# A trunk block on one core: loads of the first stage, one scale row, and the border to the FFN rearranged

## The chip, the core and the metric

The kernel runs on one core of a Trainium2 chip. The core's engines are named as the profile names them: PE (matrix unit; PEld is its weight load), DVE, ACT and POOL (elementwise engines), and SP, which issues most DMAs. The metric is the device time of one execution in microseconds (us), over three executions of each kernel. Lower is better.

## The reference

One block of a diffusion transformer, in float32, on 1024 latent tokens `x` and 256 context tokens `ctx` of width D = 1024.

```python
mod = silu(c) @ w_ada + b_ada                 # 6 x 1024: shift and scale 1, gate 1, shift and scale 2, gate 2
hc  = rmsnorm(ctx, g_pre_mix) * (1 + csc1) + csh1      # same weights, vector c_ctx
hl  = rmsnorm(x,   g_pre_mix) * (1 + sc1) + sh1
zc, zl = hc @ w_in, hl @ w_in                 # columns: q, k, v, dec, og, f, rx, rg
states = context_mixer(zc)                    # final states of GLA and RG-LRU
yl  = latent_mixer(zl, states)                # GLA (512) | 2-D DFT (256) | conv + RG-LRU (256)
x   = x + gt1 * rmsnorm(yl @ w_out, g_post_mix)
hf  = rmsnorm(x, g_pre_ffn) * (1 + sc2) + sh2
x   = x + gt2 * rmsnorm((silu(hf @ w_gate) * (hf @ w_up)) @ w_down, g_post_ffn)   # inner width 2816
```

## The kernel before

**Products.** Each float32 operand is split into a high and a low part of a reduced format (`split`: an ACT cast, line 91, and a subtraction, line 92), and `mm3` (lines 84 to 86) adds up three matmuls, high by high, high by low and low by high. So every product costs three matmuls of up to 512 columns.

**Memory and order.** Tiles come from two pools of fixed slots (`pg`, 43 of 4 KB a partition, and `hp`, 13 of 2 KB); a tile that takes a slot waits until its last user is done. A scheduler orders the instructions of each engine; an engine runs its own list strictly in that order and waits where an operand is late. All plain loads (`load`, line 70) stand in one list on SP; ACT issues the transfers of intermediate results.

**First stage.** `w_ada` holds the shift and scale of the first norm in its first 2048 columns. `ada_half(h)` (L145) loads one half of both, eight loads of 512 KB in rows of 2 KB, and multiplies them by silu of the conditioning in 64 matmuls 32x256 (L154, `ada_ps`). `columns(h)` turns the result into per-channel columns (L200 `ada_pc`, then `Acol`, `Bcol`). Both need all of a half. `transposed` (L181, `xT_ps`) turns normed tokens so that channels lie on partitions, and `modulate` scales and shifts them and splits them into `hc` (context) or `hl` (latent, two halves of 512 tokens). The order is: context normed, half 0, `hc` of its channels, the context's v (`zvc`), half 1, its k (`zkc`), then latent half 0, the context's rx (`zc`), and then the latent tokens' products: z of v for half 0 (`zn`, columns 288), half 1 modulated, z of k and rx for half 0 (`z`), v for half 1, z of k for half 1, and so on. The weights of k (`w_k`) and v (`w_v`) are split with POOL doing the subtraction.

**Rows.** `ada_row` (L664) makes one row of `mod` for all tokens: eight loads of 512 KB, each followed by a multiply-add on DVE (L671, `ada_acc`), then matmuls that sum over partitions and spread the row (L682, `row_ps`); `times_row` multiplies by a gain. It serves gate 1 (`rows[0]`) and scale 2 (`sc2`); shift 2 becomes a column instead (L676, `col_ps`). `ada_step(n)` lets n steps run at a given place of the program.

**Border to the FFN.** The FFN's three weights are multiplied by a seven-product scheme: operands a11, a12 (tokens' quarters), s1, s2, s3, s4, a22 (sums of quarters, made by `sums(n)` for block pairs n = 0 to 3) against sums of weight quarters (`t_split`). Per inner block f of 22, `first(f)` makes two of the products (24 matmuls of 512 columns, which need a11, a12 and the gate's split `b1s[f]`, made by `ff_gate(f)` and `ff_b1(f)`), and `rest(f)` the other five (60 matmuls). Eight output blocks of 128 tokens come out of `w_out` (`o_ps`); each is normed, gated, normed again (`xr`, `xn`, L1025 and L1034), transposed (L1042, `x_tr`) into `hx`, and put into the operands (`put`, a cast and a subtraction L937). POOL does part of the sums (L1071, L1074) and of the subtractions. Before the loop over f the order is sums(0), sums(1), first(0), first(1), transposes of the last block, sums(2), first(2), sums(3), the weights of f = 0, and then `rest(0)`.

Of the kernel before, what the change touches and what calls it, by code (L numbers as in the profile page):

```python
# [16 lines left out]
P = 128  # L17
# [21 lines left out]
def tile_trunk(ctx: ExitStack, tc: tile.TileContext, A: dict):  # L39
# [101 lines left out]
    sp2, sm4 = sm("sp2", 4), sm("sm4", 4)
    V.tensor_scalar_mul(sp2, sp, 2.0)
    V.tensor_scalar_mul(sm4, sp, -4.0)

    def ada_half(h):  # L145

        ps = (aux if h else mm)("ada_ps")
        for k in range(KB):
            raw = pg((P, 2, 512), name="ada_raw")
            load(raw, A["w_ada"][k * P:(k + 1) * P, 0:2 * D].rearrange("p (i n) -> p i n", i=2)[:, :, h * 512:(h + 1) * 512])  # L150
            for i in range(2):
                for j in range(2):
                    q = 32 * (2 * i + j)
                    PE.matmul(ps[q:q + 32, 0:256], s32[:, k, :], raw[:, i, j * 256:(j + 1) * 256], start=k == 0, stop=k == KB - 1)  # L154
        return ps

    Acol = pool.tile([P, KB, 2], F32, name="Acol")
    Bcol = pool.tile([P, KB, 2], F32, name="Bcol")
# [26 lines left out]
    def modulate(kps, which, hi_of, lo_of):  # L185

        for kk, ps in kps:
            f = hp((P, ps.shape[1]), name="xT")
            i = S.activation(f, ps, AF.Identity, bias=Bcol[:, kk, which:which + 1], scale=Acol[:, kk, which:which + 1])
# [4 lines left out]
    def columns(h, ps):  # L194

        sb = hp((P, 256), name="ada_sb")
        S.copy(sb, ps[:, 0:256])
        pc = (aux if h else mm)("ada_pc")[:, 0:16].rearrange("p (m q) -> p m q", q=8)
        for m in range(2):
            PE.matmul(pc[:, m], sb[:, m * P:(m + 1) * P], sel, start=True, stop=True)  # L200
        pcv = pc.rearrange("p m (i j w) -> p i j m w", i=2, j=2)

        def col4(c0):
            return sml[:, c0 + 4 * h:c0 + 4 * h + 4].rearrange("p (j m) -> p j m", j=2).unsqueeze(3).to_broadcast([P, 2, 2, 2])

        Av, Bv = (t[:, 4 * h:4 * h + 4, :].rearrange("p (j m) w -> p j m w", j=2) for t in (Acol, Bcol))
        V.tensor_add(Av, pcv[:, 1], col4(S_BSC))
        V.scalar_tensor_tensor(Av, Av, 1.0, col4(S_GPM), op0=ALU.add, op1=ALU.mult)
        V.tensor_add(Bv, pcv[:, 0], col4(S_BSH))

    load(cm, A["cmat"])
    cb = [row_block(A["ctx"], i * P) for i in range(2)]
    ada_ps = ada_half(0)
    for xb in cb:
        norm(xb)
    cT = list(transposed(cb))
# [74 lines left out]

    raws = w_N_load([(C_V, 256), (C_DEC, 32)])
    columns(0, ada_ps)
    hc = [[pg((P, 4, TC), F32R, f"hc{s}{i}") for i in range(2)] for s in range(2)]

    def mod_c(h):
        return modulate(cT[4 * h:4 * h + 4], 1, lambda kk: hc[0][kk // 4][:, kk % 4, :], lambda kk: hc[1][kk // 4][:, kk % 4, :])

    mod_c(0)
    w_v = [w_N_split(raws, G)]  # L300
    w_k_raw = [w_T_load(C_K)]
    zvc = [mm("zvc") for _ in range(2)]
# [62 lines left out]
    for m in range(2):  # L365
        v0_parts(zdt_c, m, vNc[0][:, m, :], zvc[m])
# [1117 lines left out]
```

## Time and profile before

| | before |
|---|---|
| runs | 1134.39, 1131.55, 1133.83 us; median 1133.83 |
| profiled execution | 1134.18 us, span 1132.4 us in the trace |
| busy PE, DVE, ACT, POOL | 1078.5, 810.4, 490.2, 83.6 us |
| mean granted TensorE clock | 0.979 of full speed |

The profile shows one execution. Its span is 1.8 us shorter than the time measured for it; times in the trace count from the span's start. The granted clock is given as a share of 2.4 GHz, so 0.50 in a stretch is the level of 1.2 GHz throughout.

### The profile page before, as it was taken

To read this page: it belongs to the slowest core of one execution; us is meant where nothing else is said; L and a number is where in the kernel's file an instruction comes from. 1 tells how busy PE (TensorE), PEld (TensorE's weight loads), DVE (VectorE), ACT (ScalarE), POOL (GpSimd) and SP (SyncE) were. 2 spreads that over 40 slices of the span, in tenths; PEclk is the share of its full clock that TensorE was granted. 3 is DMA by queue.
4 is the path that set the end of the run, shared out by engine and by line. 5 is a ranking of instruction groups with operands and counts; after the bars stand their busy time and mean duration, and the time that the engine had idled before them with its cause. 6 is when DMAs were issued, how large, how long until landed. Compare 5 with 4: busy or idle time off the path is not lost.

```text
span 1132.4 us, 15040 instructions
## 1 busy us (share of the span) xinstructions
PE 1078.5 (95%) x5547; PEld 900.1 (79%) x5547; DVE 810.4 (72%) x1370; ACT 490.2 (43%) x931; POOL 83.6 (7%) x93
## 2 busy tenths in 40 slices
PE   4899998999899999959999999999999999999997
PEld 2799896776689888838878888888888888888886
DVE  3474698477588466797879777768777668967794
ACT  3452675466373355663314332333323247554251
POOL 2210000103100011370000000000000000000100
PEclk8899999999999999979999999999999999999999
DMA  9802312222427222361283242424232468767572
GB/s 328 306 20 67 120 38 56 48 56 71 167 75 243 75 93 94 112 167 57 93 276 106 78 136 84 121 75 139 85 114 81 157 218 315 267 216 231 181 283 75
DMA packets 119970, 156.42 MB, mean 138 GB/s; under 512 B 8276, under 2 KB 70996, under 8 KB 119896
## 3 DMA queue, kind: packets, MB, share of 16 engines
q1 hardware_dynamic: 106536, 128.72, 34.9%
q10 hardware_dynamic: 13360, 26.75, 7.0%
q8 instruction: 43, 0.70, 0.3%
q14 instruction: 31, 0.25, 0.1%
HBM read 124.50 MB, written 28.57 MB: 135 GB/s over the span
## 4 chain that ended last, share of the span: by engine, by line
PE 83%; DVE 6%; DMA 4%; ACT 3%; issue 2%; POOL 1%; SPq 0%; DVEq 0%; POOLq 0%; ACTq 0%
PE prod L84 11%; PE prod L85 11%; PE prod L86 11%; PE dn L85 6%; PE dn L84 6%; PE dn L86 6%; PE z L84 3%; PE z L85 3%; PE z L86 3%; PE o_ps L85 3%; PE o_ps L86 3%; PE o_ps L84 3%; PE zn L85 3%; PE zn L86 3%; PE zn L84 2%; DMA wraw<-in_w_in 2%
## 5 line engine op out<-in xcount | busy, mean ns | idle before, releaser
L85 PE MATMUL dn<-dr,dl 128*128 128x512 f32 (+1 forms) x319 | 121.8, 382 | 0.0
L86 PE MATMUL dn<-dr,dl 128*128 128x512 f32 (+1 forms) x319 | 121.8, 382 | 0.0
L84 PE MATMUL dn<-dr,dl 128*128 128x512 f32 (+1 forms) x319 | 118.7, 382 | 0.0
L85 PE MATMUL zn<-w_lo,hl 128*128 128x256 f32 (+1 forms) x256 | 74.1, 292 | 0.0
L84 PE MATMUL zn<-w_hi,hl 128*128 128x256 f32 (+1 forms) x256 | 73.2, 289 | 0.0
L86 PE MATMUL zn<-w_hi,hl 128*128 128x256 f32 (+1 forms) x256 | 72.9, 288 | 0.0
L84 PE MATMUL prod<-a,b_hi 128*128 128x512 f32 x176 | 69.5, 395 | 1.4 <-ACT b_hi L91 1.4
L84 PEld LDWEIGHTS dn<-dr,dl 128*128 128x128 f32 x319 | 60.0, 188 | 11.7
L85 PE MATMUL prod<-a,b_hi 128*128 128x512 f32 x176 | 69.3, 393 | 0.0
L86 PEld LDWEIGHTS dn<-dr,dl 128*128 128x128 f32 x319 | 60.0, 188 | 11.7
L85 PEld LDWEIGHTS dn<-dr,dl 128*128 128x128 f32 x319 | 60.0, 188 | 11.5
L84 PE MATMUL prod<-s,wb_hi 128*128 128x512 f32 x176 | 68.9, 391 | 0.0
L86 PE MATMUL prod<-s,wb_lo 128*128 128x512 f32 x176 | 68.5, 389 | 0.0
L85 PE MATMUL prod<-s,wb_hi 128*128 128x512 f32 x176 | 68.5, 389 | 0.0
L86 PE MATMUL prod<-a,b_lo 128*128 128x512 f32 x176 | 67.9, 390 | 0.0
L84 PE MATMUL z<-hl,w_hi 128*128 128x512 f32 x160 | 65.5, 409 | 1.0 <-ACT on L605 1.0
L85 PE MATMUL z<-hl,w_hi 128*128 128x512 f32 x160 | 64.0, 400 | 0.0
L86 PE MATMUL z<-hl,w_lo 128*128 128x512 f32 x160 | 63.8, 399 | 0.0
L1189 ACT CAST dl<-h 128x512 fp32r<-128x512 f32 x77 | 47.8, 620 | 35.7 <-issue 20.6
L1190 DVE TENSOR_TENSOR dl<-h,dl 128x512 fp32r<-128x512 f32 x77 | 53.3, 692 | 13.6 <-ACT dl L1189 13.6
L1122 ACT CAST b<-wf_raw 128x512 fp32r<-128x512 f32 x22 | 13.7, 622 | 113.6 <-PE prod L86 105.7
L85 PE MATMUL o_ps<-wo_lo,yh 128*128 128x512 f32 x128 | 49.9, 392 | 0.0
(368 smaller groups left out, 2800.8 us busy)
## 6 DMA issues: line engine op xcount, KB each, us to landing
ada_raw<-in_w_ada SPq DMA_DIRECT2D x48, 512.0 KB, 6.3
h<-hd SPq DMA_DIRECT2D x77, 256.0 KB, 5.0
wd_raw<-in_w_down SPq DMA_DIRECT2D x77, 256.0 KB, 4.8
hd<-c ACTq DMA_DIRECT2D x55, 256.0 KB, 2.0
wf_raw<-in_w_gate SPq DMA_DIRECT2D x25, 512.0 KB, 3.9
wf_raw<-in_w_up SPq DMA_DIRECT2D x22, 512.0 KB, 4.4
wraw<-in_w_in SPq DMA_DIRECT2D x16, 512.0 KB, 4.6
xb<-in_x SPq DMA_DIRECT2D x8, 512.0 KB, 8.1
```

Of the source, the lines that this page charges most:

```text
L84: PE.matmul(out, lh, rh, start=start, stop=False)
L85: PE.matmul(out, lh, rl, start=False, stop=False)
L86: return PE.matmul(out, ll, rh, start=False, stop=stop)
L1122: S.copy(hi, u[:, 4:8])
L1189: S.copy(t[:, 0, :], raw)
L1190: V.tensor_sub(t[:, 1, :], raw, t[:, 0, :].bitcast(F32))
```

## The change

**Start.** Latent half 0 comes first. Its four blocks of x are issued on ACT's list; shift and scale are handled by blocks of 128 channels, blocks 0 and 1 alone (rows of 512 bytes), blocks 2 to 7 by pairs (rows of 1 KB); the k and rx weights come in four parts (`w4`, two loads each, rows of 1 KB). As soon as a block of channels is modulated, z of k and rx is multiplied with it (`z_block`, 12 matmuls of 512 columns). The context's work moves behind v of latent half 1. No weights are split on POOL.

```diff
+    xb0 = [pg(name="xb") for _ in range(4)]
+    for i, xb in enumerate(xb0):
+        nc.scalar.dma_start(xb, A["x"][i * P:(i + 1) * P, :])
...
+    def ada_load(b, n=1):
+        parts = [[], []]
+        for i in range(2):
+            c, kn = i * D + b * P, KB // n
+            for k0 in range(0, KB, kn):
+                raw = pg((P, kn, n * P), name="ada_raw")
+                load(raw, A["w_ada"][k0 * P:(k0 + kn) * P, c:c + n * P].rearrange("(k p) n -> p k n", p=P))
...
+    def ada_part(raws):
+        ps = aux("ada_ps")
         for k in range(KB):
...
             for i in range(2):
...
+                g = 32 * (2 * i + k % 2)
+                PE.matmul(ps[g:g + 32, 0:P], s32[:, k, :], raws[k][i], start=k < 2, stop=k >= KB - 2)
...
+    (a_raw[0],), w4_raw[0], (a_raw[1],) = ada_load(0), w4_load(0), ada_load(1)
+    for q in range(1, 4):
+        a_raw[2 * q], a_raw[2 * q + 1] = ada_load(2 * q, 2)
+        w4_raw[q] = w4_load(q)
+    v_raws = w_N_load([(C_V, 256), (C_DEC, 32)])
...
+    w4_split()
+    for b in range(KB):
+        kps = [next(x0_T)]
+        columns(b, ada_part(a_raw.pop(b)))
+        modulate(kps, 0, lambda kk: hl[0][0][kk // 2][:, kk % 2, :], lambda kk: hl[1][0][kk // 2][:, kk % 2, :])
+        if b:
+            z_block(b - 1)
+        if b % 2:
+            w4_split()
+    softplus()
+    w_v = [w_N_split(v_raws)]
+    z_block(KB - 1)
```

On PE, the matmuls of `ada_ps` stood in two long blocks. This is the list from its beginning before the change (`xT_ps` here is the context, `zvc` its v):

```order
L181 MATMUL xT_ps<-cm,xb 128x128 x4
L154 MATMUL ada_ps<-ada_raw,s_73 32x256 x4
L181 MATMUL xT_ps<-cm,xb 128x128 x12
L154 MATMUL ada_ps<-ada_raw,s_73 32x256 x28
L200 MATMUL ada_pc<-cm,ada_sb 128x8 x2
L84 MATMUL zvc<-w_hi,hc_219 128x288 x2
```

Now they stand by blocks of channels. This is the list from the columns of block 2 on (lines of the changed kernel: L197 transposes, L169 `ada_ps`, L215 `ada_pc`; `z` is k and rx of latent half 0):

```order
L215 MATMUL ada_pc<-sel_96,ada_sb 128x4
L197 MATMUL xT_ps<-cm,xb 128x128 x4
L169 MATMUL ada_ps<-ada_raw,s_83 32x128 x16
L84 MATMUL z<-hl_98,w_hi 128x512 x4
L215 MATMUL ada_pc<-sel_96,ada_sb 128x4
L197 MATMUL xT_ps<-cm,xb 128x128 x4
L169 MATMUL ada_ps<-ada_raw,s_83 32x128 x9
L85 MATMUL z<-hl_106,w_hi 128x512
```

Most of z for the blocks of one pair stands behind the ninth `ada_ps` matmul of the next pair, which reads the next pair's loads. On ACT the modulation of the last block (the second `xT` row here) stands behind the three casts of the v weights; before, the casts of the v weights stood behind the first half's modulation. Lines of the changed kernel, `ada_sb` being the copy ahead of the columns:

```order
L205 ACTIVATE xT<-xT_ps,shsc,Acol 128x512
L213 COPY ada_sb<-ada_ps 128x128
L91 CAST w_hi<-wraw 128x864 x2
L91 CAST w_hi<-wraw 128x576
L205 ACTIVATE xT<-xT_ps,shsc,Acol 128x512
```

**Rows.** Scale 2 becomes a column (`sc2`) like shift 2: eight small matmuls and a transpose of the gain in place of four `row_ps`. The scaling moves from DVE into the activation that reads the transposes, and `xn` is made on ACT. The places of the steps change, and the row of gate 2 moves from f = 3 to f = 10 and 11.

```diff
-    ada_step(9)
+    ada_step(8)
...
-    ada_step(0)
+    ada_step(1)
...
+    def scale_column(ps):
+        g8 = hp((P, P), name="g8")
+        load(g8[0:KB, :], A["g_pre_ffn"].rearrange("(k p) -> k p", p=P))
+        PE.transpose(ps[:, 16:16 + KB], g8[0:KB, :], ident[0:KB, 0:KB])
+        V.tensor_copy(sc2, ps[:, 16:16 + KB])
+        V.scalar_tensor_tensor(sc2, ps[:, 0:KB], 1.0, sc2, op0=ALU.add, op1=ALU.mult)
...
-            V.scalar_tensor_tensor(xn[:, hs], xr[:, hs], r2, sc2[:, hs], op0=ALU.mult, op1=ALU.mult)
+            S.mul(xn[:, hs], xr[:, hs], r2)
...
-                S.activation(x[:, kk, :], ps[:, k * P:(k + 1) * P], AF.Identity, bias=sh2[:, kk:kk + 1])
+                S.activation(x[:, kk, :], ps[:, k * P:(k + 1) * P], AF.Identity, bias=sh2[:, kk:kk + 1], scale=sc2[:, kk:kk + 1])
```

**Border.** The sums are made in place on `hx`, all by DVE, which also takes POOL's subtractions. Six `first` run ahead of the loop in place of three, and the gate weights of f = 0 to 5 are loaded twice (28 gate loads in place of 25). In the loop, gate and up of f + 2 are loaded at the head of step f.

```diff
-        V.tensor_add(s1, a21, a22)
-        put("s1", n, s1)
+        put("a22", n, a22)
+        V.tensor_add(a22, a21, a22)
+        put("s1", n, a22)
         yield
...
+        V.tensor_sub(a12, a12, a11)
+        put("s4", n, a12)
+        put("s3", n, a21)
...
-    EARLY = 3
+    EARLY = 6
...
+    first(2)
+    ff_gate(4)
+    ff_b1(4)
     s_last = sums(3)
     next(s_last)
-    first(2)
+    first(3)
+    ff_gate(5)
+    ff_b1(5)
     ff_gate(0)
     ff_up(0)
+    all_of(s_last)
+    first(4)
     w = t_split(0)
-    all_of(s_last)
...
+    first(5)
...
     for f in range(NFF):
...
+        if f + 2 < NFF:
+            ff_gate(f + 2)
+            ff_up(f + 2)
```

On DVE the low part of a gate's split (`b_lo`, for `first`) stood behind the sums of block pair 2 and some subtractions. Before, L1065 and L1068 are sums, L937 subtractions of `put`, L1113 adds the two products of a `first`; the `b_lo` here is that of f = 2:

```order
L1034 SCALAR_TENSOR_TENSOR xn<-xr,rs,ada_row 128x512 x2
L1113 TENSOR_TENSOR c_4681<-p_4680,prod 128x512
L1065 TENSOR_TENSOR s_4730<-hx 128x512
L1068 TENSOR_TENSOR s_4731<-s_4730,hx 128x512
L92 TENSOR_TENSOR b_lo<-wf_raw,b_hi 128x1024
```

Now the `b_lo` of f = 3 stands behind nearly all of the subtractions of pairs 0 to 2 and part of pair 3. Lines of the changed kernel, L1105 and L1106 sums, L978 subtractions, L1159 the addition in `first(2)`:

```order
L1105 TENSOR_TENSOR hx<-hx 128x512
L978 TENSOR_TENSOR s_1_4783<-hx,s_0_4781 128x2x128 x2
L978 TENSOR_TENSOR s_1_4603<-hx,s_0_4601 128x2x128
L1159 TENSOR_TENSOR c_4883<-p_4882,prod 128x512
L978 TENSOR_TENSOR s_1_4604<-hx,s_0_4602 128x2x128
L1106 TENSOR_TENSOR hx<-hx 128x512
L978 TENSOR_TENSOR s_1_4782<-hx,s_0_4780 128x2x128
L978 TENSOR_TENSOR s_1_4783<-hx,s_0_4781 128x2x128
L92 TENSOR_TENSOR b_lo<-wf_raw,b_hi 128x1024
```

From the end of the last `o_ps` to this `b_lo` DVE's list holds 16 operations of 128x512, 2 scalar-tensor-tensor of 128x512, 26 subtractions of 128x256, 2 `b_lo` and 4 of one column. From there to the low part of the first weights of `rest(0)` (`wa_lo`) it holds 12 of 128x512, 14 of 128x256 and 3 low parts of 128x1024.

## Rows read from the trace of the kernel before

**Rows 1.** Page: span; busy time, share and instructions of each engine.

```profile
span 1132.4 us, 15040 instructions
PE 1078.5 (95%) x5547; PEld 900.1 (79%) x5547; DVE 810.4 (72%) x1370; ACT 490.2 (43%) x931; POOL 83.6 (7%) x93
```

**Rows 2.** Waits of PE: line waited for, us in total, times, longest.

```profile
PE xT_ps L181 <- DVE xb L171: 10.1, 1, 10.1
PE prod L84 <- ACT wa_hi L91: 9.7, 1, 9.7
PE row_ps L682 <- DVE ada_acc L671: 5.0, 2, 4.6
PE zvc L84 <- ACT w_hi L91: 3.2, 1, 3.2
```

**Rows 3.** Windows: busy PE, PEld, DVE, ACT, POOL; PEclk, DMA share, GB/s.

```profile
0.00:4.00 4.00, 0.00 (x0) 0.00 (x0) 0.57 (x4) 1.50 (x2) 0.84 (x6) 1.00 0.47 135
4.00:8.00 4.00, 0.00 (x0) 0.00 (x0) 2.06 (x14) 3.25 (x6) 0.00 (x0) 1.00 1.01 375
24.00:28.00 4.00, 2.55 (x11) 2.21 (x11) 0.00 (x0) 1.89 (x3) 4.00 (x3) 0.50 1.05 386
32.00:36.00 4.00, 4.00 (x56) 2.61 (x58) 0.00 (x0) 0.00 (x0) 0.00 (x0) 1.00 1.11 358
44.00:48.00 4.00, 4.00 (x21) 4.00 (x20) 2.85 (x7) 1.16 (x2) 1.59 (x2) 0.55 1.11 368
60.00:113.00 53.00, 53.00 (x342) 48.88 (x341) 31.69 (x65) 20.14 (x38) 3.26 (x5) 1.00 0.14 46
700.00:800.00 100.00, 100.00 (x443) 82.81 (x442) 74.04 (x99) 31.67 (x42) 0.00 (x0) 1.00 0.31 95
```

**Rows 4.** DMA view, first 52 us: packets, bytes, mean rate.

```profile
DMA packets 12666, 17.68 MB, mean 340 GB/s; under 512 B 1790, under 2 KB 7038, under 8 KB 12663
```

**Rows 5.** Timeline of PE: start, us, line, operation; first-stage matmuls, transposes, v of half 1.

```profile
14.23 2.37 PE L154 MATMUL ada_ps<-ada_raw,s 128*32 128x256 f32 x40
...
74.37 1.04 PE L181 MATMUL xT_ps<-cm,xb 128*128 128x128 f32 x8
...
100.02 0.29 PE L84 MATMUL zn<-w_hi,hl 128*128 128x288 f32 x1
...
112.62 0.29 PE L86 MATMUL zn<-w_hi,hl 128*128 128x288 f32 x1
...
112.89 0.48 PE L84 MATMUL z<-hl,w_hi 128*128 128x512 f32 x1
```

**Rows 6.** Timeline of PE, the scale row and later the shift's columns.

```profile
301.26 1.02 PE L682 MATMUL row_ps<-ada_acc,cm 128*128 128x512 f32 x2
306.90 3.68 PE L682 MATMUL row_ps<-ada_acc,cm 128*128 128x512 f32 x4 [4.62 <-DVE ada_acc L671]
310.38 1.92 PE L613 MATMUL gate_ps<-uT,gates 128*128 128x512 f32 x4
...
365.26 1.84 PE L676 MATMUL col_ps<-cm,ada_acc 128*128 128x1 f32 x16
```

**Rows 7.** Timeline of PE, border to the FFN.

```profile
473.10 0.39 PE L86 MATMUL o_ps<-wo_hi,yl 128*128 128x512 f32 x1
...
491.65 0.79 PE L84 MATMUL prod<-a,b_hi 128*128 128x512 f32 x1 [1.08 <-ACT b_hi L91]
...
508.56 0.79 PE L84 MATMUL prod<-s,wa_hi 128*128 128x512 f32 x1 [9.74 <-ACT wa_hi L91]
```

**Rows 8.** Timeline of DVE, border to the FFN.

```profile
480.17 2.93 DVE L1025 SCALAR_TENSOR_TENSOR xr<-t,rs,xr 128x512 f32<-128x512 f32 x2
...
486.20 0.75 DVE L937 TENSOR_TENSOR s<-s,s 128x256 fp32r<-128x256 f32 x2
...
491.66 1.21 DVE L92 TENSOR_TENSOR b_lo<-wf_raw,b_hi 128x1024 fp32r<-128x1024 f32 x1
492.80 4.22 DVE L937 TENSOR_TENSOR s<-s,s 128x256 fp32r<-128x256 f32 x4
...
502.43 0.68 DVE L1113 TENSOR_TENSOR c<-p,prod 128x512 f32<-128x512 f32 x1
503.03 0.69 DVE L1068 TENSOR_TENSOR s<-s,hx 128x512 f32<-128x512 f32 x1
```

**Rows 9.** Windows, the stretch with the row of gate 2.

```profile
580.00:600.00 20.00, 19.25 (x80) 14.58 (x80) 18.45 (x23) 5.84 (x8) 0.00 (x0) 1.00 0.80 262
```

More of the change, by code (lines that the diff above doesn't have):

```diff
@@ L192, in modulate, with columns @@
         return i
[L194 to L216, printed above, removed]
+    def columns(b, ps):
+        sb = hp((P, P), name="ada_sb")
+        S.copy(sb, ps[:, 0:P])
+        pc = aux("ada_pc")[:, 0:4]
+        PE.matmul(pc, sb, sel2.rearrange("p i w -> p (i w)"), start=True, stop=True)
+        bias = sml[:, S_BSH:S_BSH + 16].rearrange("p (i k) -> p i k", i=2)[:, :, b:b + 1].to_broadcast([P, 2, 2])
+        V.tensor_add(shsc[:, b], pc.rearrange("p (i w) -> p i w", i=2), bias)
+        V.tensor_scalar(Acol[:, b, :], shsc[:, b, 1, :], 1.0, sml[:, S_GPM + b:S_GPM + b + 1], op0=ALU.add, op1=ALU.mult)
     def w_T_load(c0):
@@ new lines, in tile_trunk @@
+    softplus()
+    w_v = [w_N_split(v_raws)]
+    z_block(KB - 1)
+    load(cm[:, 1:5, :], A["cmat"][:, 1:5, :])
+    xb1 = [row_block(A["x"], i * P) for i in range(4, 8)]
+    for p in range(2):
+        S.copy(kT[p][:, 0:512], z4[p])
+    for blk in range(2):
+        conv(z4[2 + blk], uT[blk][:, 0:512], blk, 512, 64)
+    wdec_raw, wdec = hp(name="wdec_raw"), hp((P, 512), F32R, "wdec")
+    load(wdec_raw, A["wdec"])
+    S.copy(wdec, wdec_raw)
+    V.tensor_sub(wdec[32:64, :], wdec_raw[32:64, :], wdec[32:64, :].bitcast(F32))
@@ new lines, in tile_trunk @@
+    kTc, uTc = cx[:, 0:2, :], cx[:, 2:4, :]
+    for p in range(2):
+        ps = mm("zkc")
+        z_c(w_k[p], range(KB), ps)
+        S.copy(kTc[:, p, :], ps[:, 0:TC])
+    kTcs = hp((P, 2, TC), name="kTcs")
+    exchange(kTcs, kTc)
+    zdt_c = hp((P, 4, 96), name="zdt")
+    for m in range(2):
+        ps = mm("zvc")
+        for k in range(KB):
+            mm3(ps[:, 0:288], *(hc[s][k // 4][:, k % 4, m * P:(m + 1) * P] for s in range(2)), *w_v[0][k], k == 0, k == KB - 1)
+        v0_parts(zdt_c, m, vNc[0][:, m, :], ps)
@@ L407, in tile_trunk @@
+    dec_T(zdt_c, 2, zdec_c[0:96, :])
+    for blk in range(2):
+        ps = mm("zc")
+        z_c(w_rx[blk], range(KB), ps)
+        conv(ps[:, 0:TC], uTc[:, blk, :], blk, TC, TC)
     la_c = pg((P, 2, 2, TC), name="la_c")
@@ L672, in ada_row @@
             yield
-        if fn is None:
+        if not row_of:
             ps = aux("col_ps")
@@ L1391, in tile_trunk @@
         w = wn
-        if f == 3:
-            for _ in ada_row(5 * D, times_row("g_post_ffn", 0.0)):
-                pass
-            gt2 = rows[2]
+        if f == 10:
+            last_row = ada_row(5 * D, times_row("g_post_ffn", 0.0))
+            for _ in range(KB):
+                next(last_row)
+        if f == 11:
+            all_of(last_row)
+            gt2 = rows[1]
     down()
```

241 lines of the change are left out of this document (109 added, 132 removed).

## The prediction

> **What bounds the kernel now.** The page comes first: PE is busy for 1078.5 of 1132.4 us [rows 1], so what can be won is the 54 us in which PE stands idle, and what can be lost is any new idleness on PE. Next the waits of PE [rows 2]: the longest are 10.1 us at the very start, 9.7 us ahead of the first matmul of `rest(0)`, and 4.6 us ahead of the scale row. They lie in the three stages that the diff touches. Between them, PE is full: 53.00 of 53 us from 60 on, and 100.00 of 100 in the loop [rows 3], so only these three stages count, and whatever they save reaches the end undiminished. Work that PE does at half clock counts as loss too: 24 to 28 shows a granted clock of 0.50 (1.2 GHz) after a stretch with little PE work, and 44 to 48 shows 0.55 [rows 3].
>
> **Start.** I compare one point, the first k matmul of latent half 1 (112.89, [rows 5]): PE's list is the same from there in both kernels. Before it PE has the same products to do, but the order decides how much of them lies beside the loads.
>
> When are the loads in? The changed list brings 2.10 MB of x, 0.39 of constants, 8.39 of shift and scale and 2.10 of `w4`, 12.98 MB up to the last `w4`, and then 1.18 MB of v weights. By 4.0 us 0.54 MB has come (4 us at 135 GB/s). The remaining 12.44 MB take 33.2 us at the 375 GB/s of 4 to 8, and 36.6 us at 340, the mean of the first 52 us [rows 3, 4]. Rows of 512 bytes in the loop moved 95 GB/s at a DMA share of 0.31, so 306 GB/s at full share [rows 3]; at that rate it is 40.7 us. I take 340, the mean over mixed rows: the last `w4` at 40.6 and v at 44.1, with bounds 37.2 and 44.7 for `w4`.
>
> The row thus has small rows slower than large ones. The Trainium skill ("DMA: Bandwidth & Descriptors", Specifications) puts the smallest transfer at line rate at 512 bytes, so by it no load of this list is slowed, and the sum below would end at 1105.5 in place of 1109.2. Rows at both rates stand in this trace; which counts for this list, no run shows yet.
>
> Block 7's modulation stands behind the three casts of v on ACT, so the last z waits for v, not for `w4`. Cast, activation, hi copy and low subtraction of half-microsecond size take 2.5 us (46.6), and 12 matmuls of 0.226 us (100 us for 443, [rows 3]) take 2.7: z is done at 49.3. What PE must still do before the compared point is: v of both latent halves, 192 matmuls of 0.133 us (96 from 100.02 to 112.62 plus one, [rows 5]), 25.5 us; the context's v, 48 of these, 6.4; its k and rx, 96 of 256 columns, by the columns 0.118 us each, 11.3; 48 transposes at 1.04 us for 8, 0.87 where they follow one another, 5.3; small ones 2. That is 50.5 us. For handovers (accumulators copied, half 1 and the context modulated) I take 5 us, bounds 2 and 10. The point falls at 104.8, so **8 us** are won. With the fast loads and 2 us it would be 98.4 (14 won), with the slow ones and 10 us 113.8 (1 lost). ACT takes x ahead of SP's list; that only orders the same bytes.
>
> Two prices have no row. The 32x128 matmuls: forty of 256 columns took 2.37 us, 0.06 each [rows 5], so 128 of half the columns lie between half of 7.6 us and 7.6; PE has time for them while loading. And the clock: from about 15 us PE has 33 us of work beside the loads (96 z, 21.7; transposes 3.5; `ada_ps` 7.6), spread in pieces, and I assume as before that part of it runs at 1.2 GHz without moving the end, because the loads stay later.
>
> **Rows.** From the end of the first `row_ps` pair (302.28) to the gates (310.38) PE does only the scale row's four matmuls after 4.62 us of waiting, much of it at half clock [rows 6]. All 8.1 us go with the row. In its place come eight `col_ps` and a transpose later, 0.9 us by the 16 that took 1.84 [rows 6], and a wait for the last multiply-add, which I put at another 0.9; it is bounded by 0 and by the 4.6 of the old one. Won: **6.3 us**, bounds 2.6 and 7.2.
>
> **Border.** Before, the stretch from the last `o_ps` (ends 473.32 in PE's flow) to the first `rest` matmul (508.56) is 35.2 us [rows 7]; in it PE did three `first` (72 matmuls, 16.3) and 16 transposes (1.7), so 17.2 us were lost. DVE and POOL were the cause: a pair of `xr` operations took 2.93 us and four subtractions 4.22, while undisturbed a pair of subtractions takes 0.75 and an operation of 128x512 0.60 (502.43 to 503.03) [rows 8].
>
> After, PE has six `first`, 32.6 us, and 8 transposes (0.9) to do there; three of the six are only taken out of the loop. PE runs through first(0) to first(2) to 490.8. First(3) needs its `b_lo`, which stands on DVE behind 16 operations of 128x512, 2 `xr`, 26 subtractions, 2 low parts: 18 x 0.60 + 26 x 0.375 + 2 x 1.14 + 0.4 = 23.2 us from the last `o_ps` on, that is 497. So about 6 us of waiting come here, in place of the waits for `xn`, `b_hi` and `wa_hi`. Then three `first` fill PE to 513.3, and DVE's 12 x 0.60 + 14 x 0.375 + 3 x 1.14 = 15.9 us to `wa_lo` end at 512.9, so `rest(0)` follows without much of a wait at about 513.7. The loss is 513.7 - 473.3 - 32.6 - 0.9 = 6.9 in place of 17.2: **10 us** won. Bounds: nothing left but a wait of 2 us, 15 won; half clock after the wait, as at 491.65 [rows 7], and 6 us more of slow DVE, 2 won. This rests on DVE being undisturbed once POOL is silent.
>
> The 1.5 MB of gates loaded twice and the loads of f + 2 lie in a stretch where DMA has a share of 0.31 [rows 3]; nothing for them. If that cover failed, one load in a step of 19 us would cost at most its 5 us, in the first steps only.
>
> **Late row.** At f = 3 PE idles 0.75 us beside the row of gate 2 [rows 9]; at f = 10 I count **0.7 us** won, bounds 0 and 0.75.
>
> **Sum.** 8 + 6.3 + 10 + 0.7 = 25.0. The profiled execution took 1134.18, of which 1.8 lie outside the span; 1134.18 - 25.0 = 1109.2, so **1109 us**. The median of the runs shown is 1133.83, 0.35 below it, which I leave aside.
>
> **The rivals.**
> - Loads at the fast rate: at 375 GB/s `w4` and v are in 3.7 us earlier, which gives 1105.5. For it speaks 368 GB/s at 44 to 48 [rows 3], against it the loop's 306.
> - Half clock during half of the loading: twelve z of a block take 5.4 us in place of 2.7 with columns and transposes besides, longer than a block's loads (12.44 MB / 8 at 340 GB/s, 4.6 us), so PE falls behind and the start wins nothing: 1117. For it speaks the 0.50 at 24 to 28 [rows 3], and that z comes in pieces behind each landing; against it 1.00 at 32 to 36.
> - The border wins nothing: DVE now does POOL's work too, first(3) to first(5) wait for it, and 16 us are lost: 1119. For it speaks that DVE is busy there nearly all the time; against it the undisturbed durations.
> - Both of these: 1127. With the row's wait kept in another place as well (6.3 not won) it is 1133, no change: the idle time of the three stages is moved, not removed.
> - Slower: the clock stays at 0.50 from 15 us through all of the loading. The 33 us of PE work take 66, z ends at 81 to 84 in place of 49.3, some 34 us later: 1143. It decides for slower once z is more than 28 us late, that is after 77. Speaking for it is that PE waits for loads in every block; against it that PE was back at 1.00 at 32 to 36, with just such `ada_ps` work between waits.
>
> **How the numbers follow.** Forecast 0.48; fast loads 0.13; half clock in half of the loading 0.16; border without gain 0.10; both of these 0.02; no change 0.04; slower 0.07. A measurement of this kernel tells about 0.3%, 3.4 us, from no change. The first five cases lie below 1130.4: faster 0.89, same 0.04, slower 0.07. The range of 1096 to 1122 holds the first four cases; start (14 to -1) and border (15 to 2) are not at one end together, and what lies beyond with the last three cases is some 2 in 10.
>
> **What would show it.** Start: the first k matmul of half 1 near 105; the DMA rate over the first 45 us near 340; the clock between 15 and 50. Rows: `gate_ps` directly behind z, and `col_ps` without a long wait. Border: a wait of PE for `b_lo` of some 6 us near 23 us behind the last `o_ps`, DVE's subtractions at 0.36 to 0.38 each, POOL silent, and `rest(0)` without a wait of its own. The prediction is wrong if z of the first stage runs at half clock, if the doubled gate loads hold up a `first`, or if ACT, which now makes `xn` and most casts, becomes the engine that the border waits for.

## The result, and the profile after

The changed kernel takes 1118.62 us (median of 1118.52 to 1119.14, four runs) against 1133.32 (1131.55 to 1134.39): the ratio is 0.9873, 95% interval 0.9856 to 0.9890. It is 14.7 us faster; 25 were forecast. The time of 1118.6 lies in the range, 9 us above the predicted 1109.

The page of the changed kernel, span and busy times, answers to [rows 1]:

```profile
span 1116.7 us, 15346 instructions
PE 1080.1 (97%) x5696; PEld 902.0 (81%) x5696; DVE 794.6 (71%) x1394; ACT 506.3 (45%) x953; POOL 46.8 (4%) x64
```

PE does as much as before, so the 15.7 us between the spans are idle time removed: PE stands idle for 37 us in place of 54. The waits of PE, to hold against [rows 2]:

```profile
PE xT_ps L197 <- DVE xb L187: 13.0, 4, 10.2
PE prod L84 <- ACT b_hi L91: 4.2, 1, 4.2
PE z L84 <- DVE hl L206: 2.1, 4, 1.2
...
PE x_tr L1083 <- ACT xn L1075: 1.3, 1, 1.3
...
PE prod L86 <- DVE b_lo L92: 0.6, 1, 0.6
```

The waits of 9.7 for `wa_hi` and 4.6 for the scale row are gone, the wait at the very start is longer, and one of 4.2 us for a cast on ACT is new. Where on the way the time was won is seen from five points that both kernels pass, read from PE's timelines: the first v matmul behind the first stage's z, the first k matmul of half 1 (L84 `z`), the last `o_ps`, the first `rest` matmul (L84 `prod<-s,wa_hi`), and the span. The experiments below stand in the same table.

```
us                  first v  k of half 1  last o_ps  rest(0)  span
before                  -      112.89      473.10    508.56  1132.4
changed kernel        61.96    112.17      468.65    512.22  1116.7
e1_start_only         61.63    111.84      470.95    508.59  1132.6
e2_warm               58.95    109.15      465.67    510.32  1115.0
e3_rows512            63.39    113.61      470.15    513.83  1118.4
e4_gate_early         61.45    111.66      467.82    509.92  1114.6
e5_after_again        61.58    111.80      469.30    513.38  1117.9
e6_y_pg               61.53    111.74      470.20    515.30  1120.0
e7_bhi_pool           61.65    111.86      468.12    511.92  1116.4
e8_warm_gate          60.68    110.89      467.19    509.29  1114.0
e9_early7             61.28    111.50      470.51    519.45  1118.6
e10_pair              57.83    108.25      465.07    508.81  1113.3
e11_all               55.05    105.67      464.21    512.29  1111.4
```

(Before, the context's v comes first, so the first column has no entry.) From the start to the k of half 1 the change wins 0.7 us in place of 8. From there to the last `o_ps` it wins 3.7; from `o_ps` to `rest(0)` it needs 8.1 more, but has 72 more products there (16.3 us), so it wins 8.2; and behind `rest(0)` 3.0 besides those 16.3.

Each row of the table is one execution, and rows differ by chance as well. All kernels with the unedited new start (the changed kernel, e1, e4 to e7, e9) reach the first v between 61.28 and 61.96. From the k of half 1 to the last `o_ps` the changed kernel and all but e1_start_only and e6_y_pg run the same instructions, and take from 356.2 (e4_gate_early) to 359.0 us (e9_early7); the changed kernel itself takes 356.5 in one execution and 357.5 in the other (e5_after_again). So a difference of 1 us between two rows, or 2 to 3 across that stretch, shows nothing by itself. Of the four parts of the change only the start was run alone; how the rest divides among rows, border and late row is read from these points.

**The start.** Timeline of PE in the changed kernel; brackets show a pause and what ended it:

```profile
15.43 1.93 PE L169 MATMUL ada_ps<-ada_raw,s 128*32 128x128 f32 x30
...
19.20 1.94 PE L169 MATMUL ada_ps<-ada_raw,s 128*32 128x128 f32 x32
...
23.56 2.08 PE L84 MATMUL z<-hl,w_hi 128*128 128x512 f32 x4
...
33.19 1.08 PE L169 MATMUL ada_ps<-ada_raw,s 128*32 128x128 f32 x32
...
34.55 1.20 PE L84 MATMUL z<-hl,w_hi 128*128 128x512 f32 x4 [0.28 <-DVE hl L206]
...
42.64 0.64 PE L197 MATMUL xT_ps<-cm,xb 128*128 128x128 f32 x4
...
52.66 0.64 PE L197 MATMUL xT_ps<-cm,xb 128*128 128x128 f32 x4
...
61.96 0.29 PE L84 MATMUL zn<-w_hi,hl 128*128 128x288 f32 x1
```

No `ada_ps` here waits for a load. PE runs one pair of blocks in 10.0 us (42.64 to 52.66) almost without a pause, and before 27 us its matmuls take nearly twice as long as later: 1.94 against 1.08 for 32 of `ada_ps`, 2.08 against 1.20 for four z. The loads of the last pair were there before: of its four `ada_raw` loads the trace times the one issued at 29.14, which landed at 38.00, the `wraw` load issued behind all four (33.88) landed at 41.70, and PE takes the pair up at 43.21. So the loads do not set the end of the stage; PE's list does, with the chain through ACT and DVE that it waits for now and then. The windows show the rates:

```profile
4.00:8.00 4.00, 0.00 (x0) 0.00 (x0) 0.67 (x5) 3.53 (x5) 0.00 (x0) 1.00 1.05 413
...
12.00:16.00 4.00, 2.22 (x17) 1.09 (x20) 3.23 (x15) 0.05 (x1) 0.98 (x2) 1.00 1.16 312
...
24.00:28.00 4.00, 4.00 (x24) 2.50 (x24) 1.66 (x3) 1.05 (x1) 0.00 (x0) 1.00 1.10 348
```

The eleven windows up to 44 move 14.26 MB, and 14.16 are what the list holds up to the v weights; a load of the v weights issued at 38.97 landed at 44.85, and two more, 288 KB together, were issued after it. Forecast were 44.1. But the casts of v on ACT, from which the forecast reckoned the last z, start only at 54.54.

**The rows.** The gates follow z directly, at 300.06 in place of 310.38 [rows 6]:

```profile
299.83 0.39 PE L86 MATMUL z<-hl,w_lo 128*128 128x512 f32 x1
300.06 3.59 PE L654 MATMUL gate_ps<-uT,gates 128*128 128x512 f32 x8
```

The eight matmuls of the scale's column come later, without a wait ahead of them:

```profile
329.31 1.84 PE L717 MATMUL col_ps<-cm,ada_acc 128*128 128x1 f32 x16
331.09 0.22 PE L743 MATMUL col_ps<-cm,g 8*128 8x8 f32 x1
```

**The border.** Timeline of PE, to hold against [rows 7], and of ACT ahead of the cast that PE waits for:

```profile
468.65 0.47 PE L86 MATMUL o_ps<-wo_hi,yl 128*128 128x512 f32 x1
...
484.05 1.26 PE L1083 MATMUL x_tr<-cm,xn 128*128 128x128 f32 x8 [1.29 <-ACT xn L1075]
...
492.27 0.79 PE L84 MATMUL prod<-a,b_hi 128*128 128x512 f32 x1 [4.21 <-ACT b_hi L91]
...
494.93 0.80 PE L86 MATMUL prod<-a,b_lo 128*128 128x512 f32 x1 [0.59 <-DVE b_lo L92]
...
497.66 0.63 PE L86 MATMUL prod<-a,b_lo 128*128 128x512 f32 x1
...
512.22 0.39 PE L84 MATMUL prod<-s,wa_hi 128*128 128x512 f32 x1
```

```profile
487.30 2.58 ACT L977 CAST s<-hx 128x256 fp32r<-128x256 f32 x8
490.56 0.71 ACT L977 CAST s<-hx 128x256 fp32r<-128x256 f32 x2 [0.68 <-DVE hx L1105]
491.18 1.04 ACT L91 CAST b_hi<-wf_raw 128x1024 fp32r<-128x1024 f32 x1
```

PE comes to first(3) at 488.0 and goes on at 492.27, because ACT casts sums first. Its matmuls then take 0.63 in place of 0.39 until 499; the granted clock is 0.50 there, that is 1.2 GHz, and full from 500 on:

```profile
490.00:495.00 5.00, 2.14 (x5) 1.23 (x5) 5.00 (x11) 4.44 (x11) 0.00 (x0) 0.68 0.83 245
...
492.00:498.50 6.50, 5.64 (x12) 3.98 (x13) 5.58 (x11) 6.35 (x17) 0.00 (x0) 0.50 0.63 178
...
500.00:505.00 5.00, 5.00 (x24) 4.15 (x23) 4.97 (x10) 3.65 (x9) 0.00 (x0) 1.00 0.01 3
```

From then to `rest(0)`, which no longer waits, PE is full. On DVE the operations run as the forecast had them with POOL silent: the pair of `xr` takes 1.41 us where it took 2.93, four subtractions 1.42 where four took 4.22 [rows 8], and POOL has only two operations of one column between 468 and 515.

```profile
471.55 1.41 DVE L1066 SCALAR_TENSOR_TENSOR xr<-t,rs,xr 128x512 f32<-128x512 f32 x2 [0.66 <-POOL rs L121]
...
474.01 1.42 DVE L978 TENSOR_TENSOR a<-hx,a 128x256 fp32r<-128x256 f32 x4
```

### The profile page after: what moved, and what is told of

It is laid out like the page before. It is cut to its first block, busy times and chain, and to the rows that moved or that the text cites. A ratio compares the mean times of both kernels' runs of the same rounds, so it can differ in the third digit from the quotient of the medians.

```text
span 1116.7 us, 15346 instructions
## 1 busy us (share of the span) xinstructions
PE 1080.1 (97%) x5696; PEld 902.0 (81%) x5696; DVE 794.6 (71%) x1394; ACT 506.3 (45%) x953; POOL 46.8 (4%) x64
## 4 chain that ended last, share of the span: by engine, by line
PE 89%; ACT 4%; DVE 4%; issue 1%; POOL 1%; DMA 1%; DVEq 0%; POOLq 0%; ACTq 0%
PE prod L86 12%; PE prod L84 12%; PE prod L85 12%; PE dn L86 6%; PE dn L85 6%; PE dn L84 6%; PE z L84 3%; PE z L85 3%; PE z L86 3%; PE o_ps L86 3%; PE o_ps L84 3%; PE o_ps L85 3%; PE zn L85 3%; PE zn L86 3%; PE zn L84 3%
## 5 line engine op out<-in xcount | busy, mean ns | idle before, releaser
L84 PE MATMUL dn<-dr,dl 128*128 128x512 f32 (+1 forms) x319 | 118.8, 382 | 0.0
L84 PE MATMUL prod<-a,b_hi 128*128 128x512 f32 x176 | 70.0, 398 | 4.2 <-ACT b_hi L91 4.2
L84 PE MATMUL zn<-w_hi,hl 128*128 128x256 f32 (+1 forms) x256 | 73.4, 290 | 0.0
L84 PEld LDWEIGHTS dn<-dr,dl 128*128 128x128 f32 x319 | 60.0, 188 | 11.6
L84 PE MATMUL prod<-s,wb_hi 128*128 128x512 f32 x176 | 68.5, 389 | 0.0
L84 PE MATMUL z<-hl,w_hi 128*128 128x512 f32 x160 | 63.5, 419 | 3.2 <-DVE hl L206 2.1
L1192 ACT ACTIVATE c<-c 128x512 f32<-128x512 f32 x22 | 13.9, 633 | 85.4 <-DVE c L1191 82.3
```

Of the source, the lines that this page charges most:

```text
L84: PE.matmul(out, lh, rh, start=start, stop=False)
L1192: S.activation(c21, c21, AF.Silu)
```

## The experiments

The theory after the result: (1) the end of the first stage is set by PE, which begins late, runs slowly up to 27 us and has more matmul time than was priced; (2) the border is set by one cast in ACT's list and the slow matmuls behind the wait for it. The rivals: the loads set the first stage, or its gain is taken back behind it; DVE's list sets the border.

**e1_start_only.** The kernel before with nothing but the part Start of the change (its diff stands above).

```diff
+    xb0 = [pg(name="xb") for _ in range(4)]
...
+    for b in range(KB):
+        kps = [next(x0_T)]
+        columns(b, ada_part(a_raw.pop(b)))
...
```

> The kernel before with the change of the first stage alone. By the trace of the changed kernel PE reaches the first k matmul of latent half 1 at 112.17 in place of 112.89. Theory (the start itself brings next to nothing, z of the first stage ends at 62 in place of the 49 that was forecast): 0.7 us faster than before, within 1.5 us of it, about 1132.5. Rival (the start brings its 8 us, but something behind that point takes them back): the first k matmul of half 1 near 105 here, and 1125.

Measured: 1134.54 (1134.23 to 1135.47) against 1133.56; ratio 1.0008, interval 0.9999 to 1.0018. The k of half 1 comes at 111.84, the last `o_ps` 2.2 us earlier than before, and `rest(0)` at 508.59 as before: the old border takes back what little there is (PE's wait for `wa_hi` there is 10.9 us in place of 9.7). The start alone brings nothing, and the rival's 105 is not reached. What it would bring with the new border, this run does not tell.

**e2_warm.** Ten matmuls ahead of the first transposes.

```diff
+    warm = aux("warm")
+    for _ in range(10):
+        PE.matmul(warm, smask[:, 0:P], smask, start=True, stop=True)
     w4_split()
```

> The changed kernel with ten matmuls 128x512 of a constant tile ahead of PE's list, whose result nobody reads; PE has nothing else to do before 10 us. Theory (PE sets the end of the first stage, and its matmuls are slow up to 27 us because PE had stood idle: 32 of ada_ps take 1.94 us at 19.20 and 1.08 at 33.19, four z 2.08 at 23.56 and 1.20 at 34.55): the slow ones are gone, z of the first stage ends some 4 to 5 us before 61.96, about 1114. Rival 1 (the loads set the end, v lands at 44 and what follows is a chain): durations fall, the end of z and the time stay at 1118.6. Rival 2 (PE falls back to slow matmuls in the gaps of 1.1 us between the first transposes): durations stay, 1118.6.

Measured: 1118.44 (1116.77 to 1119.68), ratio to before 0.9867 (0.9853 to 0.9882), not to be told from the changed kernel's. The profiled execution, the fastest of them, has the span at 1115.0. Its PE timeline:

```profile
14.99 1.07 PE L169 MATMUL ada_ps<-ada_raw,s 128*32 128x128 f32 x30
...
18.48 1.07 PE L169 MATMUL ada_ps<-ada_raw,s 128*32 128x128 f32 x30 [0.82 <-DMA ada_raw<-in_w_ada]
...
21.07 1.21 PE L84 MATMUL z<-hl,w_hi 128*128 128x512 f32 x4
```

The slow matmuls are gone: that PE had stood idle is what made them slow. Z ends 3.0 us earlier, not 4 to 5; among other waits `ada_ps` now waits for loads (0.82 and 0.71), so up to 23 us PE and the loads are close to each other. The 3.0 us hold up to the last `o_ps`; at `rest(0)` 1.9 of them are left, and the medians show no gain.

**e3_rows512.** Blocks 2 to 7 each alone, in rows of 512 bytes.

```diff
-        a_raw[2 * q], a_raw[2 * q + 1] = ada_load(2 * q, 2)
+        (a_raw[2 * q],), (a_raw[2 * q + 1],) = ada_load(2 * q), ada_load(2 * q + 1)
```

> The changed kernel with shift and scale of blocks 2 to 7 loaded like blocks 0 and 1, each block alone in rows of 512 bytes. In the changed kernel's trace DMA moves 291 to 313 GB/s while the rows of 512 bytes are loaded and 347 with rows of 1 KB, so these 6.29 MB would take 2.9 us longer. Theory (PE sets the first stage): the rate falls to about 300, and the time stays within 1 us of 1118.6. Rival (loads set it): z of the first stage ends about 3 us later, 1121.5.

Measured: 1121.85 (1120.3 to 1122.89), ratio 0.9897 (0.9883 to 0.9912). Z ends 1.4 us later and the span is 1.7 longer, so both were half right. The window of 28 to 32 shows the rate that the expectation took from the rows of 512 bytes:

```profile
28.00:32.00 4.00, 4.00 (x22) 3.35 (x20) 1.43 (x3) 1.21 (x2) 0.00 (x0) 1.00 1.17 284
```

With 512 bytes the loads are the bound for a part of the stage: PE waits 2.32 us at 41.01 for `hl`, whose columns stand on DVE behind the split of a `w4` part, and ACT's cast for that split waited for the load:

```profile
37.04 1.05 ACT L91 CAST w_hi<-wraw 128x1024 fp32r<-128x1024 f32 x1 [3.45 <-DMA wraw<-in_w_in]
```

With rows of 1 KB that cast waits 0.44 us (at 35.06 in the changed kernel), and PE is not held up: the loads are ahead, but not by much there.

**e4_gate_early.** The gate of f = 3 ahead of the sums.

```diff
     first(0)
+    ff_gate(3)
+    ff_b1(3)
     for s in s01:
         all_of(s)
     first(1)
-    ff_gate(3)
-    ff_b1(3)
```

> The changed kernel with the load and the split of the gate of f = 3 written right behind first(0), ahead of the sums of pairs 0 and 1. On ACT its high cast moves ahead of nine operations, on DVE its low part ahead of thirteen. Theory (at the border PE waits 4.2 us for that cast at 492.27 because of where ACT's list has it, and then runs 24 matmuls at the lower clock): the wait for it and most of the slow matmuls go, 4 to 5 us, about 1114. Rival (DVE's or ACT's work sets the border anyway, and the wait comes back ahead of the next first or of rest(0)): within 1 us of 1118.6.

Measured: 1117.33 (1115.76 to 1118.78), ratio 0.9861 (0.9845 to 0.9878). The cast of f = 3 starts at 485.86, and PE waits only 0.21 us for its low part. But PE's timeline has new waits one `first` on and at `rest(0)`:

```profile
496.03 0.50 PE L84 MATMUL prod<-a,b_hi 128*128 128x512 f32 x1 [2.75 <-ACT b_hi L91]
...
509.92 0.50 PE L84 MATMUL prod<-s,wa_hi 128*128 128x512 f32 x1 [0.75 <-ACT wa_hi L91]
```

From the last `o_ps` to `rest(0)` it takes 42.1 us in place of 43.6. So of the 4 to 5 us that were expected 1.5 come at the border. The medians are 1.3 us apart, and the runs of the two kernels overlap. The wait moves on, as the rival said.

**e5_after_again.** The changed kernel on the chip of the next three.

> The changed kernel once more, on the chip of the three kernels below, as their reference: 1118.6 by every theory.

Measured: 1119.92 (1118.22 to 1121.17), ratio 0.9879 (0.9863 to 0.9896).

**e6_y_pg.** The tiles of `y_block` in 4 KB slots.

```diff
-        yh, yl = ([hp((P, 4, P), F32R, nm) for _ in range(2)] for nm in ("yh", "yl"))
+        yh, yl = ([t[:, 0:4, :], t[:, 4:8, :]] for t in [pg((P, KB, P), F32R, nm) for nm in ("yh", "yl")])
```

> The changed kernel with the tiles yh and yl in the pool of 4 KB slots again, as before the change. The matmuls of o_ps follow one another at 0.2355 us in the changed kernel and at 0.2296 before, 384 of them, 2.3 us. Theory (the smaller tiles of yh and yl cost it): o_ps back at 0.230, 2 us faster, 1116.5. Rival (it comes from something else, or the 4 KB slots are missed elsewhere): o_ps stays at 0.235 or a wait appears in its place, 1118.6 or above.

Measured: 1121.42 (1121.15 to 1121.77), ratio 0.9894 (0.9879 to 0.9908). The mean over all 384 hides what happened: a new wait of 1.96 us lies among them, and behind it nine matmuls run at half clock.

```profile
408.00 0.72 PE L84 MATMUL o_ps<-wo_hi,yh 128*128 128x512 f32 x1 [1.96 <-ACT yh L987]
...
410.22 0.63 PE L84 MATMUL o_ps<-wo_hi,yh 128*128 128x512 f32 x1
```

```profile
408.00:411.50 3.50, 3.50 (x8) 2.73 (x9) 2.86 (x5) 2.90 (x7) 0.66 (x1) 0.52 0.00 0
```

Where neither a pause nor half clock lies between two `o_ps` matmuls, they follow at 0.2274 us here, at 0.2332 in the changed kernel and in e5_after_again, and at 0.2276 before. So the theory holds for the matmuls: the tiles in 2 KB slots slow them, 2.1 us for all 384. The rival holds for the time: the wait for `yh` on ACT and its slow matmuls, some 3.8 us, cost more than that, and at the border PE waits 5.0 us for `b_hi` in place of 4.2. Why a matmul takes longer with the tiles in the smaller slots, no run shows.

**e7_bhi_pool.** On top of e4_gate_early.

```diff
     def ff_b1(f):
-        b1s[f] = split(g_raw[f], (P, KB, P), name="b1")
+        if f not in (3, 4, 5):
+            b1s[f] = split(g_raw[f], (P, KB, P), name="b1")
+            return
+        hi, lo = pg((P, KB, P), F32R, "b1_hi"), pg((P, KB, P), F32R, "b1_lo")
+        G.tensor_copy(hi, g_raw[f])
+        V.tensor_sub(lo, g_raw[f], hi.bitcast(F32))
+        b1s[f] = hi, lo
```

> The kernel of e4_gate_early with the high casts of the gates of f = 3, 4 and 5 made on POOL, which is idle there, in place of ACT. In e4_gate_early PE still waits 2.75 us for the cast of f = 4 on ACT (496.03) and 0.75 for the first weights of rest(0). Theory (ACT's list is what the border waits for): these waits go and the time falls 2 to 3 us below that of e4_gate_early, to about 1114.5. Rival (DVE's list sets the border, and POOL at work slows DVE as before the change, when a pair of 128x512 took 2.93 us): no faster than e4_gate_early, 1117.3 or above, with DVE's subtractions longer than 0.36 us beside the casts.

Measured: 1118.74 (1118.17 to 1120.32), ratio 0.9872 (0.9857 to 0.9887), no faster than e4_gate_early; in the trace `rest(0)` comes 2.0 us later than there. The cast of POOL and DVE's subtractions beside it and after it:

```profile
491.20 1.36 POOL L1017 CAST b_hi<-wf_raw 128x1024 fp32r<-128x1024 f32 x1 [1.76 <-DMA wf_raw<-in_w_gate]
```

```profile
491.58 1.59 DVE L978 TENSOR_TENSOR s<-hx,s 128x256 fp32r<-128x256 f32 x2
...
495.30 0.74 DVE L978 TENSOR_TENSOR s<-hx,s 128x256 fp32r<-128x256 f32 x2
```

Two subtractions take 1.59 us beside the cast and 0.74 without. PE now waits 5.5 us for the `b_lo` of f = 4 on DVE and none for ACT's casts: with ACT relieved DVE's list is the bound. A part of this wait is made by the edit itself: the two subtractions lose 0.85 us beside the cast, and five at 488.45 take 2.60 where five took 1.76 in e4_gate_early. That the two lists are about equally late is seen without POOL in e4_gate_early: there that `b_hi` ends at 495.97 on ACT, and DVE starts the `b_lo` at 496.01, straight behind the operation before it.

**e8_warm_gate.** The edits of e2_warm and e4_gate_early together.

```diff
+    warm = aux("warm")
...
     first(0)
+    ff_gate(3)
+    ff_b1(3)
```

> The two edits of e2_warm and e4_gate_early together. e2_warm had the last o_ps 3.0 us earlier than the changed kernel, but rest(0) only 1.9 and the end 1.7; e4_gate_early had the end 2.1 earlier. Theory (two places, their gains add up): the end 3.8 us earlier than the changed kernel, about 1114.8. Rival (ACT's and DVE's work at the border takes back what the start gains): 1116.5, with longer waits for b_hi or wa_hi at the border.

Measured: 1116.57 (1115.74 to 1120.02), ratio 0.9856 (0.9838 to 0.9874). The span is 3.9 us shorter than that of e5_after_again on the same chip, and the median 3.4, within what these runs scatter. The total is that of the sum, but its parts are not: z ends only 0.9 us earlier than in e5_after_again (60.68 against 61.58; PE is back at half clock from 57.1 to 60.5), the stretch up to the last `o_ps`, where nothing was edited, wins 1.2 more, and the border 2.0. At `rest(0)` PE waits 2.35 us for `wa_hi`, as the rival said. So this run does not show that the two gains add up.

**e9_early7.** A seventh `first` ahead of the loop.

```diff
-        if f in (4, 5):
+        if f in (4, 5, 6):
...
-    EARLY = 6
+    EARLY = 7
...
     first(4)
+    ff_gate(6)
+    ff_b1(6)
     w = t_split(0)
     first(5)
+    first(6)
```

> The changed kernel with seven first ahead of the loop in place of six, the gate of f = 6 loaded and split behind first(4). At the border DVE's list needs some 39 us of operations and took 43.3; PE has 33.5 us of work there. Theory (the border lasts as long as DVE's and ACT's lists, so a further first of 5.4 us, less the 1.7 us that its low part and its sum add on DVE, is hidden in it): rest(0) starts at most 2 us later than the 512.2 of the changed kernel though 5.4 us more of products lie before it, 3 to 4 us faster, 1116.4 on the chip of e5_after_again. Rival (the six first have no gap left that one more would fill, or its tiles hold up a load of the loop): rest(0) 5.4 us later, no change, or slower by a wait of prod in the loop.

Measured: 1119.19 (1117.95 to 1120.6), ratio 0.9879 (0.9863 to 0.9894): no change. From the last `o_ps` to `rest(0)` it takes 48.9 us, 5.4 more than the 43.6 of the changed kernel, exactly one `first`. Nothing is hidden, since PE is full from 500 on; the loss lies in the one wait ahead of first(3), which stands unchanged (4.22 at 494.14). My picture of a border as long as DVE's list was wrong.

**e10_pair.** Both blocks of a pair multiplied at once.

```diff
-    def ada_part(raws):
+    def ada_part(raws, n):
...
-                PE.matmul(ps[g:g + 32, 0:P], s32[:, k, :], raws[k][i], start=k < 2, stop=k >= KB - 2)
+                PE.matmul(ps[g:g + 32, 0:n * P], s32[:, k, :], raws[k][i], start=k < 2, stop=k >= KB - 2)
...
-        columns(b, ada_part(a_raw.pop(b)))
+        if b in a_raw:
+            n = 2 if b > 1 else 1
+            ps = ada_part(a_raw.pop(b), n)
+            for j in range(n):
+                columns(b + j, ps[:, j * P:(j + 1) * P])
```

> The changed kernel with shift and scale of a pair of blocks multiplied together, 16 matmuls 32x256 in place of 32 of 32x128 for a pair. Loads and bytes stay. By the rows of before forty records of 256 columns take 2.37 us, so 32 for a pair 1.9 in place of 2.2, and changes between kinds of matmul on PE's list get fewer. Theory (PE sets the first stage): z of the first stage ends 1 to 3 us before 61.96 and the time falls by 1 to 2 us. Rival (loads or the chain of columns and modulation set it): no earlier, or later, since both blocks' columns now wait for the whole pair.

Measured: 1115.33 (1115.12 to 1116.98), ratio 0.9849 (0.9833 to 0.9866); all four runs lie below those of e9_early7 on the same chip. Same loads, fewer matmuls:

```profile
22.68 1.19 PE L84 MATMUL z<-hl,w_hi 128*128 128x512 f32 x4
...
32.03 2.17 PE L169 MATMUL ada_ps<-ada_raw,s 128*32 128x256 f32 x32
...
50.11 0.51 PE L215 MATMUL ada_pc<-sel,ada_sb 128*128 128x4 f32 x4
50.48 0.64 PE L197 MATMUL xT_ps<-cm,xb 128*128 128x128 f32 x4
```

Z ends 4.1 us before that of the changed kernel, more than expected, and 3.4 of it reach the span. Nothing in the loads has changed, so they did not set the end. But the reason that was expected is the smaller part: 32 records of 256 columns take 2.17 us, no less than twice the 1.08 of 32 with 128. And a part is not the edit's: here PE's matmuls are at full speed from 21.3 us on, four z at 22.68 in 1.19 us, while the changed kernel's are slow up to 27, though PE's list up to 22 us is the same. From the sums of what each kind of matmul takes in these two kernels, in e2_warm and in e11_all, I estimate 1.6 of the 4.1 us for this. Clearer is e11_all (below) beside e2_warm, where none of these matmuls is slow: with the pairs z ends at 55.05 in place of 58.95, and PE's waits for `hl` fall from 2.6 us to nothing. So the pairs win mainly by fewer waits for modulated tokens and fewer changes between kinds of matmul.

**e11_all.** e2_warm, e4_gate_early, e9_early7 and e10_pair together.

```diff
+    warm = aux("warm")
...
+                PE.matmul(ps[g:g + 32, 0:n * P], s32[:, k, :], raws[k][i], start=k < 2, stop=k >= KB - 2)
...
+    EARLY = 7
```

> Warm matmuls at the start, pairs multiplied together, the gate of f = 3 early, and seven first. If the first stage is PE's and the border DVE's, the gains of e2_warm (3 us at the last o_ps), e9 (3 to 4) and e4 add up to 6 to 8 us below the changed kernel, 1112. Rival (the border takes back whatever the start gains, as in e2_warm and e8_warm_gate): 3 to 4 us, 1115.5.

Measured: 1113.87 (1113.02 to 1115.72), ratio 0.9834 (0.9819 to 0.9848), the lowest median of all, though not clear of e10_pair's, and 0.4% below the changed kernel by the ratios. Z ends 6.9 us earlier, the span is 5.3 shorter; 2.1 us are lost between the k of half 1 and the last `o_ps`, where nothing was edited and the rows of the table scatter by as much. It lies between theory and rival.

## Why the prediction was half right

**Sign and places: right.** Faster, by removing idle time of PE in the three stages and not by less work. The profile shows each of them. The total falls nearer to 1117 and 1119, the times of two rivals, than to 1109: it cannot tell which of them holds, the places can; and it lies in the range although the largest single error, 7 us at the start, is in it.

**The start: wrong, 8 us forecast, 0.7 won.** The failed step is "The 32x128 matmuls [...] PE has time for them while loading", and with it z's end at 49.3, which was reckoned from the landing of v. The loads came as forecast (v at about 45), but PE was not waiting for them: z ended at 61.96, 12.7 us later. Three things made PE's list the bound. It was priced at 33 us of work from 15 us on, which would already have ended at 48, within a microsecond or two of the loads' chain, so there was no margin, and the text left the comparison out. The `ada_ps` term was too small: an instruction is two records in the trace, so the change has 256 records, not 128, and they took 13.1 us in place of at most 7.6 (10.9 in e2_warm, where none of them is slow, so most of the excess is the count):

```profile
L169 PE MATMUL ada_ps<-ada_raw,s 128*32 128x128 f32 x256 | 13.1, 323 | 0.0
L84 PE MATMUL z<-hl,w_hi 128*128 128x512 f32 x32 | 10.9, 451 | 2.1 <-DVE hl L206 2.1
```

(Groups of PE up to 62 us in the changed kernel: busy us, mean ns, idle before.) And PE's slow matmuls up to 27 us do move the end of z, against "without moving the end, because the loads stay later": without them z ends 3.0 us earlier (e2_warm). Changes between kinds of matmul and waits for `hl` (2.1 us) had no term at all. The loads' bound of 306 GB/s, called that of rows of 512 bytes, was read off a mixture: 4.22 of the 9.52 MB moved from 700 to 800 are transfers of another queue, in rows of 2 KB; no step hung on it. The rival "half clock during half of the loading" gave this effect, no gain at the start and 1117 in all, for nearly this reason: slow matmuls for a part of it and too much work for PE for the rest. The other side of the sum was better than forecast: from z's end to the k of half 1 it took 50.2 us, the 50.5 of work with no handover lost, where 5 us were put.

**The rows: the term came out right, 6.3, by luck.** Between the k of half 1 and the last `o_ps`, PE's time up to the next matmul, summed over its timeline, falls by 8.25 us for `row_ps` (11.16 to 2.91) and rises by 1.9 for `col_ps` (1.70 to 3.48, and 0.15 for the gain's transpose), 6.3 in all. Two errors cancel in it: the eight matmuls of the column were put at 0.9, half of sixteen records, but eight matmuls are sixteen records and take 1.8, the same mistake as with `ada_ps`; and the wait that was put at 0.9 did not come. The stretch won only 3.7 (2.7 in e5_after_again): eight transposes more lie in it (0.8, moved from the border), and the 384 matmuls of `o_ps` take 90.3 us in place of 88.2. That was not forecast. It comes from the tiles yh and yl, which the change puts into smaller slots: with them in 4 KB slots again the matmuls follow as before (e6_y_pg).

**The border: the place was right, the engine was not, and the size was 7.3 in place of 10.** Reckoned as in the prediction, 43.3 us from the end of the last `o_ps` less 32.6 for six `first` and 0.9 for transposes leaves 9.8 lost, in place of 6.9 forecast and 17.2 before. The waits add up to 6.1 where some 6 were expected; 4.8 of them (4.21 and 0.59) are at the place that was named, in first(3), and 1.29 are for the transposes of the last block. The mis-sized term is the matmuls behind the wait: up to 499 they ran at half clock, 3 us that the prediction had only in its bound. Who was late was wrong too: it was ACT's cast `b_hi`, with DVE's `b_lo` 0.6 us behind it, since DVE's list waits for ACT's casts of sums. That ACT becomes the engine the border waits for is one of the signs by which the prediction called itself wrong. The rival by which DVE sets the border is refuted in its strong form (e9_early7), but e7_bhi_pool shows that DVE comes next.

**The late row: mis-sized, 3.0 in place of 0.7.** Behind `rest(0)`, the old kernel began with matmuls at half clock after its wait of 9.74 (0.63 each up to 511.71), about 1.6 us that are gone now, beside the 0.75 of the row; what makes the remaining 0.6 was not traced. I had not counted what a removed wait takes with it.

The sum of the four, 0.7, 3.7, 8.2 and 3.0, is the 15.7 us between the spans.

## What to carry to other kernels

When loads and a compute engine both run through a stage, work out both ends and take the later one, and when they lie within a few us of each other, count the pauses between kinds of instructions as well: here removing the waits for loads only handed the stage to the engine. Count matmuls in the trace's own unit: one of `ada_ps` or `col_ps` is two records here. Price a wait with the slow matmuls that follow it, and leave these out before you compare what a matmul takes in two kernels: one mean over a pause and slow matmuls hid what e6_y_pg was made to show. At this border a wait that was taken from the head of one list came back one step later, on the same list or another engine's (e4_gate_early, e7_bhi_pool), so such an edit was worth only the distance to the second-latest operand.

## What the runs showed of the hardware

After PE had stood idle for 10 us, its matmuls took almost double up to 27 us (four z in 2.08, later 1.20; from one z matmul to the next 0.43 us up to 27.2, 0.23 from 27.9 on), and ten matmuls ahead of them removed this (e2_warm). The windows up to 27 us give the granted clock as 1.00, but that is no reading: the trace's first record of the clock, one of full speed, stands at 27.61 us, where the matmuls become fast, and a window without a record is given as 1.00. In e10_pair the first record stands at 21.04, and the matmuls are fast from 21.3 on. The Trainium skill ("TensorE: Matmul & The Clock Gate", "What's actually happening") has PE at 1.2 GHz by default and after idleness, and the durations agree.

DMA moved 413 GB/s with rows mostly of 4 KB (4 to 8), 348 with rows of 1 KB (24 to 28), 312 with rows of 1 KB and 512 bytes mixed (12 to 16), and 284 with rows of 512 bytes (28 to 32 in e3_rows512), at shares over 1.0 each time. The Trainium skill ("DMA: Bandwidth & Descriptors", Specifications) has line rate from 512 bytes on; here the rate still grows beyond that, by a fifth from 512 bytes to 1 KB.

Beside a cast of 128x1024 on POOL two subtractions of 128x256 on DVE took 1.59 us, and 0.74 without it (e7_bhi_pool).
